# Two-layer hybrid decoder trunk on one core: column vectors of the second layer summed by VectorE, four products in place of sixteen transposes, and eight units in place of four kept back at the end

## The chip, the cores and the metric

The kernel runs on one core of a Trainium2 chip. A core has a matrix engine (TensorE, PE in the profile, with its weight loads as PEld), three engines for elementwise work (VectorE or DVE, ScalarE or ACT, GpSimd or POOL) and SyncE (SP), which issues most of the DMA transfers. Every engine has an instruction row of its own and works through it in order; the engines meet at semaphores only. The metric is the device time of one execution in microseconds (us): of the kernel before there are three runs with a median of 2212.91, from 2211.6 to 2215.46.

## The reference

Two layers over 256 tokens of 2048 numbers, all float32. Layer 0 mixes tokens with forgetting attention, layer 1 with windowed attention; each mixer is followed by a gated feed-forward part with 5632 columns. Before each of the four parts the tokens are modulated by a scale and a shift, and behind it the output is multiplied by a gate, added and normalised. Scales, shifts and gates come from one conditioning vector `c` through one large weight per layer (2048 x 12288, 100 MB each). The change touches these.

```python
def reference(x, c, ..., ada_w, ada_b, ...):
    c_act = jax.nn.silu(c)
    for i in range(DEPTH):                                   # DEPTH = 2
        mod = c_act @ ada_w[i] + ada_b[i]
        sh1, sc1, g1, sh2, sc2, g2 = jnp.split(mod[:, None, :], 6, axis=-1)
        h = x * (1.0 + sc1) + sh1
        y = fox_attention(h, ...) if i % 2 == 0 else swa_attention(h, ...)
        x = layer_norm(DEEPNORM_ALPHA * x + (1.0 + g1) * y, ln_mix_g[i], ln_mix_b[i])
        h = x * (1.0 + sc2) + sh2
        y = conv_ffn(h, ...)
        x = layer_norm(DEEPNORM_ALPHA * x + (1.0 + g2) * y, ln_ffn_g[i], ln_ffn_b[i])
    return x
```

## The kernel before

**Units.** All large weights stream through the core once, in pieces of 256 rows x 512 columns (512 KB); the text calls a piece a unit, and there are 728: 96 + 32 for layer 0's mixer (input and output projection), 264 for its feed-forward part (to U392), 40 + 32 for layer 1's mixer (to U464), 264 for the last feed-forward part. Each unit takes four steps. SyncE issues its load into `w` (L265, ten buffers in the pool that it shares with other loads). ScalarE copies it to `wh` in a type of fewer bits that TensorE multiplies faster (CAST, L268). VectorE subtracts to get the rest, `wl = w - wh` (L279). TensorE then multiplies three times, `wh` with the high part of the tokens, `wl` with the high part, `wh` with the low part (all from L75), which together give nearly the accuracy of float32. `wh` and `wl` have four buffers each.

With the tokens stationary (`x_mm`), a unit is twelve products of 512 columns: for each half of the tokens (t = 0 and 1, 128 tokens each) and each 128 rows, three. That is the form in the output and down projections, into the PSUM tiles `xs`. With the weights stationary (`w_mm`), a unit is 24 products of 256 columns (tiles `ws`).

**The background: conditioning vectors.** Ten of the twelve vectors of scales, shifts and gates are made beside the stream, in the order of `ada_list`: (layer, number) with numbers 0 and 1 for the mixer's shift and scale, 2 for its gate, 3 and 4 for the feed-forward part's, 5 for its gate. Each takes 32 loads `wa` of 128 x 1024 (L391) and 32 multiply-adds on VectorE into `acc` (L395 for the first, L397 for the rest), which leave 128 partial sums for each of the 2048 columns. How fast this goes is set by a rate: `ada_tick` adds the rate once per unit and takes one step of the generator `ada_vector` (to its next `yield`) for each whole number; `ada_need` takes all steps that are left when a vector is needed. What is left to do with `acc` depends on the vector:

- A gate is needed as a row in all partitions. It is split into `ah` and `al` (L84, L85), multiplied by ones, and copied into `gate`.
- A scale or shift is needed as a column block `cv` of 128 x 16. TensorE transposes the sixteen 128 x 128 blocks of `acc` in four groups of four (L439, `sm<-ident,acc`), ScalarE sums each transposed block along its row into `tot` (L443, sixteen accumulations), and VectorE adds the bias (L425). The four steps of four blocks are a `yield` apart; there are five yields in all. So are the columns of (1,0), (1,1), (1,3) and (1,4) made, and two of layer 0.

**Turns between parts.** `between` stands after each part: it waits for the vectors that the next part needs, merges the norm's weights into them, normalises the tokens (L655 on ScalarE for t = 0, L657 on VectorE for t = 1), transposes them (L496) and modulates them into `hH` and `hL`. The residual before it is L632 (product times gate), L634 (add to `x`), L639, L642, L644 (statistics), L645 (power -1/2 on GpSimd) and L638. TensorE waits for this chain at each turn. The text calls the one between layer 0 and layer 1 (after U392) the first turn, and the one between layer 1's output projection and its feed-forward part (after U464) the second.

**The end of a projection.** `x_mm_end` changes the order in the last n units: their products for t = 0 run first, the units are kept, and the products for t = 1 follow for all n. So the residual and the statistics of t = 0 can run beside the rest. n is 2 in layer 0's last down projection and 4 in layer 1's. Behind the latter stands the end of the program: eight normalising steps for each half (L1180, L1181) and the stores (L1182).

**What sets the order.** The program is written as one stream of units with steps put between them (`then`, `defer`, `run_post`, `tick`). The framework then orders each engine's row; what is wrapped in `pin` keeps its order against the other pinned instructions.

Of the kernel before, what the change touches and what calls it, by code (L numbers as in the profile page):

```python
# [10 lines left out]
F32 = mybir.dt.float32  # L11
F32R = mybir.dt.float32r
I32 = mybir.dt.int32
AF = mybir.ActivationFunctionType
ALU = mybir.AluOpType
# [26 lines left out]
def hybrid_trunk(ctx: ExitStack, tc: tile.TileContext, a: dict, out: bass.AP):  # L42
# [22 lines left out]
    def bank(name="sm"):  # L65
        return psp.tile([P, 512], F32, tag="ps", name=name)
# [66 lines left out]
    onesr = cst.tile([P, P], F32R, name="onesr")  # L133
    nc.vector.tensor_copy(onesr, ones)

    NF = 2 * DFF // P
    HR = ROPE_DIM // 2
    lcol = cst.tile([P, 4, DEPTH, KC], F32, name="lcol")
# [36 lines left out]
    def rotary():  # L175
# [2 lines left out]
        posr = tp.tile([NT, P], I32, tag="t", name="posr")  # L178
        nc.gpsimd.dma_start(posr, a["positions"].rearrange("b (t p) -> (b t) p", p=P))
        yield  # L180
        nc.vector.tensor_scalar_mul(nsink, sink, -1.0)
        posf = tp.tile([NT, P], F32, tag="t", name="posf")
        nc.vector.tensor_copy(posf, posr)
# [31 lines left out]
    def then(fn, alone=False):  # L215

        if alone:
            lone.add(fn)
        work.append(fn)
        if len(work) == 1 and not ahead[0]:  # L220
            settle()
# [35 lines left out]
        while post:  # L257
            run_post()

    def stream(wsrc, row0, col, ks, use):  # L260

        for kc in ks[::2]:
            r0 = (row0 + kc) * P
            w = wtile()
            pin(nc.sync.dma_start(w, wsrc[r0:r0 + 2 * P, col:col + WB].rearrange("(k p) f -> p k f", p=P)), False)  # L265
            h = hl.tile([P, 2, WB], F32R, tag="wh", name="wh")
            l = hl.tile([P, 2, WB], F32R, tag="wl", name="wl")
            pin(nc.scalar.copy(h, w), False)  # L268

            def go(kc=kc, h=h, l=l):  # L270
                ahead[0] -= 1
                run_post()
                use(kc, h, l)
                if feeds:
                    feeds.pop(0)()
                tick()

            def residual_(w=w, h=h, l=l, go=go):
                pin(nc.vector.tensor_tensor(l, w, f32(h), op=ALU.subtract), behind[0] > 0)  # L279
                behind[0] -= 1  # L280
                del residuals[go]

            ahead[0] += 1
            weights.add(go)
            residuals[go] = residual_
            work.append(go)
            settle(2)
# [25 lines left out]
    def w_mm(ps, kc, h, l, last=KC - 1, first=0):  # L313

        for i in range(2):
            for f in range(4):
# [3 lines left out]
                mm(o, wh, hL[:, kc + i, :], skip_group_check=True)  # L320
                mm(o, wl, hH[:, kc + i, :], stop=kc + i == last, skip_group_check=True)

    def x_stationary(wsrc, col, k0, nk, stat, end=0):

        ps = x_banks()
        use = x_mm_end(ps, stat, nk, end) if end else lambda kc, h, l: x_mm(ps, kc, h, l, stat, nk - 1)
        stream(wsrc, k0, col, list(range(nk)), use)
        return ps

    def w_stationary(wsrc, col):  # L330
# [42 lines left out]
    def ada_vector(l, v):  # L373
# [55 lines left out]
        if (l, v) in HELD:  # L429
            held.append((sums, finish))  # L430
            ada["held"] = not HELD[l, v]
            ready_cols.add((l, v))
        else:

            tot = sp.tile([P, KC], F32, tag="tot", bufs=1, name="tot")
            for k in range(0, KC, 4):
# [38 lines left out]
    def ada_need(l, v):  # L475
        while (l, v) not in cols and (l, v) not in gates and (l, v) not in ready_cols:
            ada_step()
# [272 lines left out]
    def out_proj(oT, full, w_o, l):  # L750
# [9 lines left out]
            stream(w_o, 0, d * WB, ks, use)  # L760

        for i, ks in enumerate((range(0, 8), range(8, 12))):
            then(lambda i=i: ada.update(rate=(1.3, 0.65)[l]))
            for d in range(2):
                part(d, list(ks))
        then(lambda: (ada_need(l, 2), ada.update(rate=(1.3, 0.75)[l])))
        for d in range(D // WB):
            if d < 2:
                part(d, list(range(12, KC)))
# [316 lines left out]
    def conv_ffn(l):  # L1086
# [37 lines left out]
        for si, (b0, b1) in enumerate(sbs):  # L1124
# [19 lines left out]

            then(ready)
            for d in range(D // WB):
                ps = x_stationary(w_dn, d * WB, b0 * 4, (b1 - b0) * 4, stat, (2, 4)[l] if si > 0 and d == D // WB - 1 else 0)
                then(lambda ps=ps, d=d, si=si: defer(residual(ps, d, gates[l, 5], si == len(sbs) - 1)),
                     si > 0 and d == D // WB - 1)
        then(lambda: (flush(), ada.update(gate_free=True)), True)  # L1150
# [58 lines left out]
```

## Time and profile before

| what | value |
|---|---|
| runs: median (lowest to highest) | 2212.91 us (2211.6 to 2215.46), 3 runs |
| profiled execution, device time | 2215.89 us |
| its span | 2214.0 us |
| TensorE busy | 2164.3 us, 98% |
| VectorE busy | 1792.8 us, 81% |
| ScalarE busy | 1159.6 us, 52% |
| GpSimd busy | 19.0 us, 1% |
| data moved by DMA | 602.98 MB, mean 272 GB/s |
| granted TensorE clock | 0.992 of full speed |

The span is the time between the first and the last instruction that the profile shows. A busy share is an average over the whole program; what counts for a change is the stretch in which it stands. Lines such as `1464.83 0.39 PE L75 MATMUL xs<-wh,hH 128*128 128x512 f32 x1` are read: start in us from the span's begin, duration, engine, line of the kernel, operation, output and inputs by the program's names, sizes, and how many of the kind in a row are put together. `[0.83 <-DVE mv L644]` says how long the engine had been idle ahead of it and which instruction ended that.

### The profile page before, as it was taken

Reading aid. Unit: us, or ns where it says so; the run is one execution under the profiler, and the core shown is the slowest. Engines: PE = TensorE matmul, PEld = TensorE weight load, DVE = VectorE, ACT = ScalarE, POOL = GpSimd, SP = SyncE. Lnnn points to the kernel's source line nnn. Section 1 sums busy time; section 2 is a strip of 40 time slices with the busy share of each in tenths; the row PEclk is TensorE's granted clock in tenths of the full one; section 3 lists DMA queues with packets and bytes.
Section 4 is the critical chain, followed back from the end, with each engine's and each line's share of the span. In section 5 each row is a group of like instructions: output and inputs, shape, how many; then the busy total and the mean of one; then the engine's idle time right before and its main releaser. Section 6 shows DMA issues by size and latency. Waiting matters only on the chain. (4 is left out here: it accounts for less than half of the span.)

```text
span 2214.0 us, 38357 instructions
## 1 busy us (share of the span) xinstructions
PE 2164.3 (98%) x14915; PEld 1976.7 (89%) x14915; DVE 1792.8 (81%) x2459; ACT 1159.6 (52%) x1841; POOL 19.0 (1%) x48
## 2 busy tenths in 40 slices
PE   6999999999999999999999999999999999999997
PEld 5999888789999988999987877789999988999986
DVE  6879998989978979799798888789888655666756
ACT  3435656465565543655644677555555533555532
POOL 0000000000000000000000000000000000000000
PEclk9999999999999999999999999999999999999999
DMA  9999998979978989899797676678888566666663
GB/s 334 368 352 366 351 352 298 327 257 323 349 234 300 322 312 385 260 311 322 251 354 290 201 240 206 208 257 295 281 264 270 187 194 195 192 195 195 191 195 108
DMA packets 274246, 602.98 MB, mean 272 GB/s; under 512 B 21062, under 2 KB 29960, under 8 KB 273552
## 3 DMA queue, kind: packets, MB, share of 16 engines
q1 hardware_dynamic: 273008, 595.85, 79.6%
q0 software_dynamic: 1056, 4.69, 0.6%
q8 instruction: 116, 1.90, 0.3%
q14 instruction: 66, 0.54, 0.1%
HBM read 598.37 MB, written 2.10 MB: 271 GB/s over the span
## 5 line engine op out<-in xcount | busy, mean ns | idle before, releaser
L268 ACT CAST wh<-w 128x1024 fp32r<-128x1024 f32 x728 | 765.3, 1053 | 790.0 <-PE ws L75 284.5
L75 PE MATMUL ws<-hH,wh 128*128 128x256 f32 x6656 | 1153.3, 278 | 4.6 <-ACT hH L84 2.1
L279 DVE TENSOR_TENSOR wl<-w,wh 128x1024 fp32r<-128x1024 f32 x728 | 887.6, 1222 | 325.3 <-ACT wh L268 308.5
L75 PEld LDWEIGHTS ws<-hH,wh 128*128 128x128 f32 x6656 | 1012.1, 189 | 9.0 <-ACT hH L84 2.3
L75 PE MATMUL ws<-hH,wl 128*128 128x256 f32 x3328 | 918.6, 277 | 4.3 <-DVE wl L279 4.0
L75 PEld LDWEIGHTS ws<-hH,wl 128*128 128x128 f32 x3328 | 628.5, 189 | 6.0 <-DVE wl L279 5.9
L75 PE MATMUL xs<-wh,gT 128*128 128x512 f32 x1408 | 435.3, 389 | 0.0
L75 PEld LDWEIGHTS xs<-wh,gT 128*128 128x128 f32 x1408 | 264.3, 188 | 54.7
L75 PE MATMUL xs<-wl,gT 128*128 128x512 f32 x704 | 273.9, 389 | 0.0
L75 PE MATMUL xs<-wh,hH 128*128 128x512 f32 x704 | 235.9, 401 | 0.0
L397 DVE SCALAR_TENSOR_TENSOR acc<-wa,cact,acc 128x1024 f32<-128x1024 f32 x180 | 228.4, 1278 | 0.0
L397 DVE SCALAR_TENSOR_TENSOR acc<-wa,cactp,acc 128x1024 f32<-128x1024 f32 x128 | 162.3, 1278 | 0.3 <-DMA acc<-in_ada_b_dram 0.3
L75 PEld LDWEIGHTS xs<-wh,hH 128*128 128x128 f32 x704 | 131.3, 188 | 29.4 <-issue 0.7
L75 PEld LDWEIGHTS xs<-wl,gT 128*128 128x128 f32 x704 | 132.2, 188 | 27.4
L75 PE MATMUL xs<-wl,hH 128*128 128x512 f32 x352 | 138.7, 395 | 2.5 <-DVE wl L279 2.5
L1093 ACT ACTIVATE u<-ws,ccol 128x256 f32<-128x256 f32 x176 | 96.7, 562 | 58.5 <-PE ws L75 43.3
L75 PE MATMUL xs<-wh,oT 128*128 128x512 f32 x384 | 126.2, 397 | 0.8 <-ACT oT L84 0.8
L1094 DVE SCALAR_TENSOR_TENSOR u<-ws,ccol,u 128x255 f32<-128x255 f32 x176 | 82.6, 477 | 14.9 <-ACT u L1093 14.7
L75 PEld LDWEIGHTS xs<-wh,oT 128*128 128x128 f32 x384 | 72.1, 188 | 16.6 <-ACT oT L84 1.2
L1096 DVE SCALAR_TENSOR_TENSOR u<-ws,ccol,u 128x254 f32<-128x254 f32 x176 | 83.1, 477 | 2.2
L75 PEld LDWEIGHTS xs<-wl,hH 128*128 128x128 f32 x352 | 66.5, 189 | 17.5 <-DVE wl L279 4.3
L576 DVE SCALAR_TENSOR_TENSOR oacc<-wo,cact,oacc 128x1024 f32<-128x1024 f32 (+1 forms) x68 | 73.3, 1078 | 8.3 <-DMA wo<-in_ada_w_dram 7.1
(220 smaller groups left out, 1280.4 us busy)
## 6 DMA issues: line engine op xcount, KB each, us to landing
w<-in_ffn_w_up_dram SPq DMA_DIRECT2D x352, 512.0 KB, 4.7
wa<-in_ada_w_dram SPq DMA_DIRECT2D x320, 512.0 KB, 5.6
w<-in_ffn_w_down_dram SPq DMA_DIRECT2D x176, 512.0 KB, 4.9
w<-in_fox_w_in_dram SPq DMA_DIRECT2D x96, 512.0 KB, 6.9
wo<-in_ada_w_dram SPq DMA_DIRECT2D x48, 512.0 KB, 9.0
w<-in_swa_w_in_dram SPq DMA_DIRECT2D x40, 512.0 KB, 4.6
w<-in_fox_w_o_dram SPq DMA_DIRECT2D x32, 512.0 KB, 6.2
w<-in_swa_w_o_dram SPq DMA_DIRECT2D x32, 512.0 KB, 4.8
```

What stands on the lines that cost most here:

```text
L75: return nc.tensor.matmul(o, lhsT, rhs, start=start, stop=stop, **kw)
L268: pin(nc.scalar.copy(h, w), False)
L279: pin(nc.vector.tensor_tensor(l, w, f32(h), op=ALU.subtract), behind[0] > 0)
L397: pin(nc.vector.scalar_tensor_tensor(ac, wo, (cactp if row else cact)[:, k:k + 1], ac, op0=ALU.mult, op1=ALU.add), True)
L576: nc.vector.scalar_tensor_tensor(acc, w[:, k], cact[:, kc:kc + 1], acc, op0=ALU.mult, op1=ALU.add)
L1093: nc.scalar.activation(u, pf, AF.Identity, bias=cw(CW, f), scale=cw(2, f))
L1094: nc.vector.scalar_tensor_tensor(u[:, 1:], pf[:, :S - 1], cw(1, f), u[:, 1:], op0=ALU.mult, op1=ALU.add)
L1096: nc.vector.scalar_tensor_tensor(u[:, 2:], pf[:, :S - 2], cw(0, f), u[:, 2:], op0=ALU.mult, op1=ALU.add)
```

## The change

There are four parts.

**Column vectors of layer 1.** For (1,0), (1,1), (1,3) and (1,4) the sixteen transposes on TensorE and the sixteen accumulations on ScalarE fall away. VectorE instead turns `acc` in place, in four pieces of 128 x 512: its transpose turns every 32 x 32 block within itself (L448 of the changed kernel). Two reductions of 128 x 1024 to 128 x 32 then sum each row of each block (L452) into `red`, 128 x 64. That leaves, for each column, four partial sums that stand 32 partitions apart and in a group of partitions of their own. Four float32 products with the stationary `fold` bring them together and put them in the partitions where `cv` has them, all into one bank of 128 x 16; the last line (L434) adds the bias, straight from the bank. A column vector has now seven yields behind its multiply-adds where it had five. Layer 0's two vectors stay as they were.

**`fold`.** A constant of 128 x 4 x 128, zeros (GpSimd's memset) and ones, made at the program's start by four small reductions of the identity on VectorE.

**Eight units at the end.** In layer 1's last down projection `x_mm_end` keeps eight of ten units. Eight pairs of `wh` and `wl` don't fit the four buffers, so four pairs are put in the region of `hH` and `hL`, which nobody reads any more at that place (`spares`).

**Rates.** In layer 1's output projection the background's rate is 0.75 per unit instead of 0.65 in its first part, and 1.1 instead of 0.75 behind that.

```diff
+    fold = cst.tile([P, 4, P], F32, name="fold")
+    nc.gpsimd.memset(fold, 0.0)
...
+        for q in range(4):
+            nc.vector.tensor_reduce(fold[:, q, q * 32:(q + 1) * 32], ident.rearrange("p (a i) -> p i a", a=4),
+                                    axis=AX.X, op=ALU.add)
...
-    def stream(wsrc, row0, col, ks, use):
+    def stream(wsrc, row0, col, ks, use, spare={}):
...
-            h = hl.tile([P, 2, WB], F32R, tag="wh", name="wh")
-            l = hl.tile([P, 2, WB], F32R, tag="wl", name="wl")
+            h, l = spare.get(kc) or (hl.tile([P, 2, WB], F32R, tag=n, name=n) for n in ("wh", "wl"))
...
+    def spares(nk):
+        t = [hpad[:, 56 + i * 2 * WB:56 + (i + 1) * 2 * WB].rearrange("p (a f) -> p a f", a=2) for i in range(8)]
+        return {nk - 16 + 2 * i: (t[2 * i], t[2 * i + 1]) for i in range(4)}
+
     def x_stationary(wsrc, col, k0, nk, stat, end=0):
...
-        stream(wsrc, k0, col, list(range(nk)), use)
+        stream(wsrc, k0, col, list(range(nk)), use, spares(nk) if end == 8 else {})
...
         else:
+
+            if l > 0:
+
+                for b in range(D // 512):
+                    r = acc[:, b * 512:(b + 1) * 512]
+                    nc.vector.transpose(r, r)
+                    yield
+                red = sp.tile([P, D // 32], F32, tag="red", bufs=1, name="red")
+                for b in range(2):
+                    nc.vector.tensor_reduce(red[:, b * 32:(b + 1) * 32],
+                                            acc[:, b * 1024:(b + 1) * 1024].rearrange("p (c j) -> p c j", j=32),
+                                            axis=AX.X, op=ALU.add)
+                    yield
+                tb = bank()
+                for q in range(4):
+                    mm(tb[:, :KC], fold[:, q, :], red.rearrange("p (k q) -> p q k", q=4)[:, q, :],
+                       start=q == 0, stop=q == 3)
+                yield
+                ps.append(tb)
+                finish()
+                ada["held"] = v == 4
+                return
 
             tot = sp.tile([P, KC], F32, tag="tot", bufs=1, name="tot")
...
-            then(lambda i=i: ada.update(rate=(1.3, 0.65)[l]))
+            then(lambda i=i: ada.update(rate=(1.3, 0.75)[l]))
...
-        then(lambda: (ada_need(l, 2), ada.update(rate=(1.3, 0.75)[l])))
+        then(lambda: (ada_need(l, 2), ada.update(rate=(1.3, 1.1)[l])))
...
-                ps = x_stationary(w_dn, d * WB, b0 * 4, (b1 - b0) * 4, stat, (2, 4)[l] if si > 0 and d == D // WB - 1 else 0)
+                ps = x_stationary(w_dn, d * WB, b0 * 4, (b1 - b0) * 4, stat, (2, 8)[l] if si > 0 and d == D // WB - 1 else 0)
```

The change adds lines, so that the same statement has another number behind it: the multiply-add L397 is L406, the subtraction L279 is L284, the residual's L632, L634, L639, L642, L644 and L638 are L663, L665, L670, L673, L675 and L669, the normalising L657 is L688, and the end's L1180 and L1181 are L1211 and L1212. Three places in VectorE's row show what moves.

The first is the last residual of layer 0, at the first turn; `xs` is the projection's bank, `mv` and `rs` the statistics of a half. Before:

```order
L632 TENSOR_TENSOR t<-xs,gate 128x512
L634 TENSOR_TENSOR x<-x,t 128x512
L639 BN_STATS stats<-x 128x6
L642 BN_AGGR mv<-stats 128x2
L644 TENSOR_SCALAR mv<-mv 128x1
L632 TENSOR_TENSOR t<-xs,gate 128x512
L634 TENSOR_TENSOR x<-x,t 128x512
L638 SCALAR_TENSOR_TENSOR rs<-mv,rs 128x1
L639 BN_STATS stats<-x 128x6
L642 BN_AGGR mv<-stats 128x2
```

After:

```order
L663 TENSOR_TENSOR t<-xs,gate 128x512
L665 TENSOR_TENSOR x<-x,t 128x512
L406 SCALAR_TENSOR_TENSOR acc<-wa,cactp,acc 128x1024
L670 BN_STATS stats<-x 128x6
L663 TENSOR_TENSOR t<-xs,gate 128x512
L673 BN_AGGR mv<-stats 128x2
L665 TENSOR_TENSOR x<-x,t 128x512
L675 TENSOR_SCALAR mv<-mv 128x1
L85 TENSOR_TENSOR al<-acc,ah 128x512
L669 SCALAR_TENSOR_TENSOR rs<-mv,rs 128x1
L670 BN_STATS stats<-x 128x6
L673 BN_AGGR mv<-stats 128x2
```

A multiply-add of the gate (1,2) and the first `al` of its split now stand inside this chain, and the two halves are woven into each other.

The second is layer 1's output projection, where the sums of (1,4) run. Before:

```order
L639 BN_STATS stats<-x 128x6
L397 SCALAR_TENSOR_TENSOR acc<-wa,cact,acc 128x1024
L634 TENSOR_TENSOR x<-x,t 128x512
L279 TENSOR_TENSOR wl<-w,wh 128x1024
L639 BN_STATS stats<-x 128x6
L397 SCALAR_TENSOR_TENSOR acc<-wa,cact,acc 128x1024
L279 TENSOR_TENSOR wl<-w,wh 128x1024
L397 SCALAR_TENSOR_TENSOR acc<-wa,cact,acc 128x1024
L279 TENSOR_TENSOR wl<-w,wh 128x1024
L397 SCALAR_TENSOR_TENSOR acc<-wa,cact,acc 128x1024
L279 TENSOR_TENSOR wl<-w,wh 128x1024 x2
```

After:

```order
L670 BN_STATS stats<-x 128x6
L406 SCALAR_TENSOR_TENSOR acc<-wa,cact,acc 128x1024
L665 TENSOR_TENSOR x<-x,t 128x512
L284 TENSOR_TENSOR wl<-w,wh 128x1024
L670 BN_STATS stats<-x 128x6
L406 SCALAR_TENSOR_TENSOR acc<-wa,cact,acc 128x1024 x2
L284 TENSOR_TENSOR wl<-w,wh 128x1024
L406 SCALAR_TENSOR_TENSOR acc<-wa,cact,acc 128x1024
L284 TENSOR_TENSOR wl<-w,wh 128x1024
L406 SCALAR_TENSOR_TENSOR acc<-wa,cact,acc 128x1024
L284 TENSOR_TENSOR wl<-w,wh 128x1024
L406 SCALAR_TENSOR_TENSOR acc<-wa,cact,acc 128x1024
```

Between two subtractions there are now two multiply-adds at one place, and one between all others, so that the vector's sums stand earlier among the units.

The third is the program's end. Before:

```order
L279 TENSOR_TENSOR wl<-w,wh 128x1024 x5
L632 TENSOR_TENSOR t<-xs,gate 128x512
L634 TENSOR_TENSOR x<-x,t 128x512
L639 BN_STATS stats<-x 128x6
L642 BN_AGGR mv<-stats 128x2
L644 TENSOR_SCALAR mv<-mv 128x1
L1180 SCALAR_TENSOR_TENSOR x<-x,mv,ln 128x512 x2
L1181 SCALAR_TENSOR_TENSOR x<-x,rs,ln 128x512 x2
L1180 SCALAR_TENSOR_TENSOR x<-x,mv,ln 128x512
L632 TENSOR_TENSOR t<-xs,gate 128x512
L1181 SCALAR_TENSOR_TENSOR x<-x,rs,ln 128x512
L634 TENSOR_TENSOR x<-x,t 128x512
```

After:

```order
L284 TENSOR_TENSOR wl<-w,wh 128x1024 x3
L663 TENSOR_TENSOR t<-xs,gate 128x512
L665 TENSOR_TENSOR x<-x,t 128x512
L670 BN_STATS stats<-x 128x6
L673 BN_AGGR mv<-stats 128x2
L675 TENSOR_SCALAR mv<-mv 128x1
L1211 SCALAR_TENSOR_TENSOR x<-x,mv,ln 128x512 x2
L1212 SCALAR_TENSOR_TENSOR x<-x,rs,ln 128x512 x2
L1211 SCALAR_TENSOR_TENSOR x<-x,mv,ln 128x512 x2
L1212 SCALAR_TENSOR_TENSOR x<-x,rs,ln 128x512 x2
L663 TENSOR_TENSOR t<-xs,gate 128x512
L665 TENSOR_TENSOR x<-x,t 128x512
```

All eight normalising steps of the first half (t = 0) now stand ahead of the second half's last residual; before, a part of them stood there.

## The prediction

> **What bounds the kernel now.** I read the page first (busy shares, granted clock), then the busy time in windows of 20 us, then the groups by form, and last the timeline at the five places that the change touches. All times are us.
>
> ```profile
> PE 2164.3 (98%) x14915; PEld 1976.7 (89%) x14915; DVE 1792.8 (81%) x2459; ACT 1159.6 (52%) x1841; POOL 19.0 (1%) x48
> ...
> PEclk9999999999999999999999999999999999999999
> ```
>
> TensorE is the bound, at full clock. The windows say where it has company; their columns are the stretch, its length, then busy time and instruction count of PE, PEld, DVE, ACT, POOL, then clock, DMA share and GB/s:
>
> ```profile
> 780.00:800.00 20.00, 20.00 (x97) 16.52 (x97) 12.68 (x13) 11.98 (x34) 0.00 (x0) 1.00 0.89 323
> 900.00:920.00 20.00, 20.00 (x178) 20.00 (x177) 12.55 (x16) 13.68 (x38) 0.00 (x0) 1.00 0.73 233
> 1080.00:1100.00 20.00, 20.00 (x174) 19.87 (x174) 10.40 (x13) 11.90 (x28) 0.58 (x1) 1.00 0.71 237
> 1200.00:1220.00 20.00, 18.66 (x85) 14.22 (x85) 14.75 (x28) 11.65 (x16) 1.10 (x2) 1.00 0.31 100
> 1420.00:1440.00 20.00, 20.00 (x90) 16.57 (x89) 20.00 (x23) 8.30 (x8) 0.00 (x0) 1.00 0.76 246
> ```
>
> At 780, 900 and 1080, where the sums of three of the four column vectors stand, TensorE has no gap and VectorE has 7 to 9 us free. At 1200 (first layer to second) TensorE waits. At 1420 (second layer's output projection) both are full. So a product taken off TensorE at the first three is worth its whole time there; at the last two it depends on VectorE.
>
> **The change, part by part.** "Unit" below is one weight piece of 512 KB: one CAST, one L279 subtraction, twelve 512-column products.
>
> *Turned sums off TensorE.* Four vectors lose 16 TensorE transposes each (L439), in groups of four. What one group costs, and the price list for VectorE:
>
> ```profile
> 1464.83 0.39 PE L75 MATMUL xs<-wh,hH 128*128 128x512 f32 x1
> 1465.06 0.60 PE L439 MATMUL sm<-ident,acc 128*128 128x128 f32 x4
> 1465.41 0.48 PE L75 MATMUL xs<-wh,hH 128*128 128x512 f32 x1
> ```
> ```profile
> L279 DVE TENSOR_TENSOR wl<-w,wh 128x1024 fp32r<-128x1024 f32 x728 | 887.6, 1222 | 325.3 <-ACT wh L268 308.5 <-DMA w<-in_ffn_w_down_dram 5.9 <-DMA wa<-in_ada_w_dram 5.8
> L397 DVE SCALAR_TENSOR_TENSOR acc<-wa,cact,acc 128x1024 f32<-128x1024 f32 x180 | 228.4, 1278 | 0.0
> L632 DVE TENSOR_TENSOR t<-xs,gate 128x512 f32<-128x512 f32 x48 | 32.1, 686 | 15.5 <-PE xs L75 15.3
> L705 DVE CUSTOM_DVE_ANT_0 pr<-S,mask,nsink 128x128 f32<-128x128 f32 x32 | 11.0, 345 | 0.0
> ```
>
> A product starts 0.23 after the one before it (1464.83 to 1465.06), so a unit of twelve takes about 2.7. The group pushes the next product back by 0.35 (1465.06 to 1465.41) and stretches it by 0.09 (0.48 against 0.39): 0.44. Of the 16 groups the last of the fourth vector came after the projection's last product, where TensorE waits anyway; 15 x 0.44 = **-6.6**. ScalarE's 64 accumulations go too, and cost nothing but at the second turn below.
>
> *Four small products per vector.* 16 in all, f32, 128x128 stationary, 16 columns. No such form is in the trace; the nearest is the one-column sum:
>
> ```profile
> 78.69 1.84 PE L75 MATMUL cps<-ones,oacc 128*128 128x1 f32 x16
> 80.40 0.25 PE L75 MATMUL cps<-cact,wo 128*128 128x1 f32 x1
> ...
> 20.63 1.87 PE L75 MATMUL cps<-ones,oacc 128*128 128x1 f32 x8 [0.51 <-DVE oacc L576]
> ```
>
> (80.40 - 78.69) / 16 = 0.107 each at speed, 1.87 / 8 = 0.234 in the opening. A group of four is 0.43, and I add 0.1 for the stretched product behind it, as with the transposes: 4 x 0.53 = **+2.1**; ends 1.7 and 16 x 0.234 = 3.7. I take the low row since these products stand in the running stream. [...]
>
> *Turned blocks and row sums on VectorE*, 4 + 2 per vector. Not in the trace. The turned block (128x512) I take as the 0.69 of L632, the row sum (128x1024) as the 1.22 of L279, which have the same columns: 4 x 0.69 + 2 x 1.22 = 5.2 per vector. The low end is nothing, the high end the dearest per column among the wide rows, L705 with 345 / 128 = 2.7 ns: 1.38 and 2.76, 11.0 per vector. The first three vectors have 7.3, 7.5 and 9.6 of VectorE time free (windows above), so 5.2 is hidden; the fourth is counted with the projection. The four reductions that build `fold` stand between the first loads of the program, where VectorE waits for DMA; 0.
>
> *Order: first layer's end.* Each vector now yields twice more, so the gate vector's sums end later. The order puts one L397 (L406 now) and one `al` subtraction into VectorE's row between the two halves' residuals, ahead of the statistics. The tail before:
>
> ```profile
> 1206.20 0.69 DVE L634 TENSOR_TENSOR x<-x,t 128x512 f32<-128x512 f32 x1
> ...
> 1207.95 0.15 DVE L644 TENSOR_SCALAR mv<-mv 128x1 f32<-128x1 f32 x1
> 1208.20 0.69 DVE L632 TENSOR_TENSOR t<-xs,gate 128x512 f32<-128x512 f32 x1
> ...
> 1209.54 0.15 DVE L638 SCALAR_TENSOR_TENSOR rs<-mv,rs 128x1 f32<-128x1 f32 x1
> ...
> 1210.68 0.15 DVE L644 TENSOR_SCALAR mv<-mv 128x1 f32<-128x1 f32 x1
> 1211.50 1.92 DVE L657 TENSOR_SCALAR x<-x,mv,rs 128x512 f32<-128x512 f32 x4 [0.66 <-POOL rs L645]
> ```
>
> Replay: the L397 runs 1206.8 to 1208.1 behind L634, so the second L632 starts at 1208.6 instead of 1208.20; the first L644 moves from 1207.95 to 1210.0 since three instructions of the other half now stand before it; then `al` to 1210.8; L638 must wait for GpSimd's power, which starts after L644 and so is ready at about 1210.9; L639 to L644 follow, and L657 starts at 1212.85. Behind it wait the x transposes, and TensorE: **+1.35**. Ends: 0.4 (only the later L632) and 2.0 (L397 and `al` in full).
>
> *Order: second layer's projection.* With the rates 0.75 and 1.1 the (1,4) vector's pieces come sooner.
>
> ```profile
> 1420.29 0.68 DVE L632 TENSOR_TENSOR t<-xs,gate 128x512 f32<-128x512 f32 x1
> ...
> 1434.39 1.27 DVE L397 SCALAR_TENSOR_TENSOR acc<-wa,cact,acc 128x1024 f32<-128x1024 f32 x1
> 1435.58 1.22 DVE L279 TENSOR_TENSOR wl<-w,wh 128x1024 fp32r<-128x1024 f32 x1
> ```
> ```profile
> 1438.47 0.39 PE L75 MATMUL xs<-wl,oT 128*128 128x512 f32 x1
> ```
>
> From 1420.29 VectorE runs without a gap to the subtraction of 1435.58, whose result TensorE reads first at 1438.47: 1.67 in hand. Up to that subtraction the order now holds two more L397 (1.19 from its start to the next, 1434.39 to 1435.58), and one before the residuals that makes them 0.35 later: its end moves from 1436.80 to 1439.3, past 1438.47: TensorE waits **+0.9**. After it the subtractions regain ground (one L397 and one subtraction take 2.3, a unit of TensorE 2.7); the turned blocks and row sums then stand among six subtractions, the tightest of which ends about 0.5 before it is needed. Ends: 0, if the row starts 0.9 sooner, and 3, if sums cost 1.5 each more and that 0.5 goes too.
>
> *Second turn.*
>
> ```profile
> 1472.30 0.15 DVE L644 TENSOR_SCALAR mv<-mv 128x1 f32<-128x1 f32 x1
> 1472.55 0.56 POOL L645 TENSOR_TENSOR rs<-mv,mhalf 128x1 f32<-128x1 f32 x1 [0.83 <-DVE mv L644]
> ...
> 1473.56 0.18 DVE L425 SCALAR_TENSOR_TENSOR cv<-tot,acol 128x16 f32<-128x16 f32 x1 [1.10 <-ACT sm L443]
> 1473.65 0.54 DVE L657 TENSOR_SCALAR x<-x,mv,rs 128x512 f32<-128x512 f32 x1
> ```
>
> L657 stood behind L425, which waited for ScalarE's last accumulation. The vector is now finished before the projection ends, and L657 can follow the power as at the first turn (0.82 after L644 started): 1473.12, **-0.5**. Next in line is the power itself.
>
> *Eight units kept.* Half the tokens finish early; what is left when TensorE ends:
>
> ```profile
> 2194.78 0.69 DVE L632 TENSOR_TENSOR t<-xs,gate 128x512 f32<-128x512 f32 x1 [3.13 <-PE xs L75]
> ...
> 2197.25 0.15 DVE L644 TENSOR_SCALAR mv<-mv 128x1 f32<-128x1 f32 x1
> ...
> 2199.11 0.62 PE L75 MATMUL xs<-wh,gT 128*128 128x512 f32 x2
> ...
> 2199.79 0.39 PE L75 MATMUL xs<-wh,gT 128*128 128x512 f32 x1
> ...
> 2200.63 0.68 DVE L632 TENSOR_TENSOR t<-xs,gate 128x512 f32<-128x512 f32 x1
> ...
> 2204.77 0.15 DVE L644 TENSOR_SCALAR mv<-mv 128x1 f32<-128x1 f32 x1
> ...
> 2208.82 1.41 DVE L1181 SCALAR_TENSOR_TENSOR x<-x,rs,ln 128x512 f32<-128x512 f32 x2
> ```
>
> Three products take 2199.79 - 2199.11 = 0.68, a kept unit's second half (six) 1.36. The first half now ends 8 x 1.36 = 10.9 before TensorE's last product instead of 5.4. It needs 2.6 (L632 to L644) and eight normalising steps of about 0.66, 5.3, so it is done with over 2 to spare. Then the second half's L632 starts with the last product's end (2200.2, not 2200.63) and reaches the end of L644 in 2.6 plus 0.1 for L638: 2202.9 instead of 2204.92, and what follows is unchanged: **-2.0**. The first halves consume weights at 1.36 per unit, above VectorE's 1.22; four of the eight pairs lie in the dead `hH` area and are cast ahead, so I cost that at 0. Without that cover up to 1.36 per late unit would be lost.
>
> Sum: -6.6 + 2.1 + 1.35 + 0.9 - 0.5 - 2.0 = **-4.75**. The profiled execution took 2215.89 (span 2214.0 and 1.89 around it), 2.98 over the median of the runs, 2212.91; I put the difference on the median: **2208.2**.
>
> **The rivals.**
> *VectorE late in the projection, or the end not gained.* For it: the full window at 1420. Against it: the row regains ground. With 3 in place of 0.9 the sum is -2.65, 2210.3; without the -2.0 it is -2.75, 2210.2. Within 0.2% either way.
> *Dear turned blocks and row sums; slower.* At the fourth vector every microsecond beyond 0.5 added to its four turned blocks and two row sums is TensorE's. At the high end, 11.0 instead of 5.2, that is 5.3 lost and 2213.5, no change; the kernel becomes slower by 0.2% (4.4) only if the six cost some 15 instead of 5.2, so about threefold. [...]
> *Cheaper than summed.* The first turn at 0.4 and no wait in the projection: -6.6, 2206.3.
> *A late load in the first turn.* Loads are held by buffers:
>
> ```profile
> 1197.66 20.47 SPq L265 DMA_DIRECT2D w<-in_swa_w_in_dram  x4
> ```
>
> Had the L397 in the tail to wait for its piece, the statistics would wait too; but its load stands about seven before these four. I leave it inside the first rival.
>
> **How the numbers follow.** About 0.2% (4.4) is what a measurement of this kernel can tell from no change. The summed case 0.60 (its spread crosses that bound: 0.48 beyond it, 0.12 within), the cheaper one 0.10, less gained 0.22, slower 0.08: faster 0.58, same 0.34, slower 0.08. Low end: no wait, 0.4 at the turn, products 1.7: -7.0, 2205.9, and from it the 1.3 by which the fastest run shown (2211.6) lies below the median: 2204.5. High end: products 3.7, turn 2.0, wait 3: -0.4, 2212.5.
>
> **What would show it.** After the change: no L439 after 500 and 16 products of 16 columns near 0.11; turned blocks near 0.69, row sums near 1.22; L657 at the first turn 1.3 later after TensorE's last product than before, at the second 0.5 sooner; one wait of TensorE near 1.0 for a `wl` in the projection; the chain's last part 8 after TensorE's last product instead of 10. The prediction is wrong if turned blocks take over 1.4, if `wl` waits exceed 3, or if TensorE waits in the last eight units.

## The result, and the profile after

The changed kernel takes 0.9987 of the time before, with a 95% interval of 0.9981 to 0.9993: medians of 2210.65 us (21 runs, 2208.81 to 2214.61) and 2215.11 (21 runs beside them, 2211.28 to 2219.55). By the ratio that is 2.9 us less, between 1.6 and 4.2: faster, but by less than the 0.2% that the prediction set as its bound, and by less than its 4.75. (The medians lie 4.5 apart and the means 3.5; the text goes by the ratio, since it comes with an interval.) The profiled execution took 2210.2 (span 2208.4).

Page of the changed kernel, busy time by engine, then the windows (columns as in the prediction):

```profile
PE 2158.4 (98%) x14883; PEld 1970.1 (89%) x14883; DVE 1810.2 (82%) x2487; ACT 1138.4 (52%) x1713; POOL 20.0 (1%) x49
```
```profile
780.00:800.00 20.00, 20.00 (x90) 16.58 (x89) 16.74 (x18) 7.39 (x7) 0.00 (x0) 1.00 0.90 309
900.00:920.00 20.00, 20.00 (x179) 20.00 (x178) 18.88 (x23) 10.59 (x14) 0.00 (x0) 1.00 0.82 270
1420.00:1440.00 20.00, 18.99 (x84) 15.38 (x83) 20.00 (x22) 6.66 (x7) 0.00 (x0) 1.00 0.84 260
```

VectorE filled up by 4 to 6 us where the first two vectors are summed, and TensorE still has no gap there; at 1420 TensorE now lacks 1.01. The new VectorE operations (durations in ns, least, median, most):

```profile
L448 DVE STREAM_TRANSPOSE acc<-acc x16: 669/704/709, 783.8 to 1450.8; 128x512 f32<-128x512 f32 x16
L452 DVE TENSOR_REDUCE red<-acc x8: 1177/1210/1216, 789.9 to 1454.9; 128x32 f32<-128x1024 f32 x8
```

That is 4 x 0.70 + 2 x 1.21 = 5.2 per vector, as summed. To see where time went, both traces are cut where TensorE changes over: the first group of idle-time products (`spin`) of each turn starts directly behind the last product of the part before. Timeline of the kernel before at the three turns and at its last product:

```profile
471.14 2.10 PE L75 MATMUL spin<-mask,ident 128*128 128x384 f32 x6
...
1208.01 2.10 PE L75 MATMUL spin<-mask,ident 128*128 128x384 f32 x6
...
1470.06 2.10 PE L75 MATMUL spin<-mask,ident 128*128 128x384 f32 x6
...
2199.79 0.39 PE L75 MATMUL xs<-wh,gT 128*128 128x512 f32 x1
```

And of the changed one:

```profile
468.78 2.10 PE L75 MATMUL spin<-mask,ident 128*128 128x384 f32 x6
...
1202.55 2.10 PE L75 MATMUL spin<-mask,ident 128*128 128x384 f32 x6
...
1467.15 2.10 PE L75 MATMUL spin<-mask,ident 128*128 128x384 f32 x6
...
2196.27 0.39 PE L75 MATMUL xs<-wh,gT 128*128 128x512 f32 x1
```

| stretch (us) | before | after | difference |
|---|---|---|---|
| start and layer 0's mixer, to 471.14 | 471.1 | 468.8 | -2.4 |
| layer 0's feed-forward part, three column vectors | 736.9 | 733.8 | -3.1 |
| first turn and layer 1's mixer | 262.1 | 264.6 | **+2.5** |
| second turn and last feed-forward part | 729.7 | 729.1 | -0.6 |
| last product to the end of the span | 14.2 | 12.1 | -2.1 |

The first row is not the change's alone: in the thirteen traces of this study the start took from 465.7 to 471.1 us. The four others repeat: a second trace of the changed kernel has them within 0.25 of the first. They add up to -3.3, inside the 1.6 to 4.2 of the measured ratio.

### The profile page after: what moved, and what is told of

Same layout as the page of the kernel before. It is cut to its first block, busy times and chain, and to the rows that moved or that the text cites. A ratio compares the mean times of both kernels' runs of the same rounds, so it can differ in the third digit from the quotient of the medians.

```text
span 2208.4 us, 38187 instructions
## 1 busy us (share of the span) xinstructions
PE 2158.4 (98%) x14883; PEld 1970.1 (89%) x14883; DVE 1810.2 (82%) x2487; ACT 1138.4 (52%) x1713; POOL 20.0 (1%) x49
## 4 chain that ended last, share of the span: by engine, by line
PE 82%; DVE 10%; issue 3%; ACT 2%; DMA 2%; SPq 0%; POOL 0%; DVEq 0%; ACTq 0%; POOLq 0%
PE ws L75 46%; PE xs L75 32%; DVE acc L406 3%; DVE wl L284 3%; DMA wo<-in_ada_w_dram 1%; ACT wh L273 1%; DMA w<-in_fox_w_in_dram 1%; PE sm L527 1%; PE cps L75 1%; DVE oacc L607 1%; PE S L75 1%; DVE pr L736 0%; PE sm L75 0%; PE o L75 0%; ACT pr L740 0%
## 5 line engine op out<-in xcount | busy, mean ns | idle before, releaser
L284 DVE TENSOR_TENSOR wl<-w,wh 128x1024 fp32r<-128x1024 f32 x724 | 881.7, 1220 | 300.2 <-ACT wh L273 274.0
L75 PE MATMUL xs<-wh,gT 128*128 128x512 f32 x1376 | 425.2, 389 | 0.0
L75 PEld LDWEIGHTS xs<-wh,gT 128*128 128x128 f32 x1376 | 258.3, 188 | 53.7
L75 PE MATMUL xs<-wl,gT 128*128 128x512 f32 x688 | 267.7, 389 | 0.0
L406 DVE SCALAR_TENSOR_TENSOR acc<-wa,cact,acc 128x1024 f32<-128x1024 f32 x180 | 227.9, 1276 | 0.0
L406 DVE SCALAR_TENSOR_TENSOR acc<-wa,cactp,acc 128x1024 f32<-128x1024 f32 x128 | 162.2, 1276 | 0.6 <-DMA acc<-in_ada_b_dram 0.6
```

Of the source, the lines that this page charges most:

```text
L75: return nc.tensor.matmul(o, lhsT, rhs, start=start, stop=stop, **kw)
L406: pin(nc.vector.scalar_tensor_tensor(ac, wo, (cactp if row else cact)[:, k:k + 1], ac, op0=ALU.mult, op1=ALU.add), True)
```

## The experiments

The theory after this comparison: the time is the sum of the parts, and the gain was eaten at three places, by the four products, by the first turn, and by a wait for `wl` in layer 1's output projection (the wait is there, but not for `wl`: see the old rates). Rivals are given with each.

**The end alone.** The kernel before, with the eight kept units.

```diff
-  ... (2, 4)[l] if si > 0 and d == D // WB - 1 else 0)
+  ... (2, 8)[l] if si > 0 and d == D // WB - 1 else 0)     (with spares(), as in the change)
```

> The kernel before with the eight kept units (and the four pairs in the dead region) alone. Distance from the start of TensorE's last product to the end of the span: 14.25 us before, 12.14 after. Theory (the end is a part of its own, worth what its chain of waits shows): 12.1 here too, no wait of TensorE in the last ten units, everything ahead as before, so 2.1 faster, a ratio of 0.9990. Rival (the eight units make TensorE or VectorE wait for buffers, and the two traces differ there by the start of the program only): the distance falls to 12.1, but TensorE's products of the last ten units take over 1 us longer than before, and the time does not change.

Ratio 0.9994 (0.9985 to 1.0003). TensorE's last product and the last normalising steps in its timeline:

```profile
2199.08 0.39 PE L75 MATMUL xs<-wh,gT 128*128 128x512 f32 x1
```
```profile
2199.51 0.69 DVE L635 TENSOR_TENSOR t<-xs,gate 128x512 f32<-128x512 f32 x1 [2.94 <-PE xs L75]
...
2206.03 1.41 DVE L1184 SCALAR_TENSOR_TENSOR x<-x,rs,ln 128x512 f32<-128x512 f32 x2
```

From the last product to the end of the span (2211.3) it is 12.2, the stretch ahead of it 729.75 against 729.73: the end is worth 2.1 and costs nothing. VectorE had idled 2.94 before the last residual, so it is not late. The ratio alone is too wide to show 0.1%; the trace does.

**Five steps per vector.**

```diff
                     nc.vector.transpose(r, r)
-                    yield
+                    if b % 2:
+                        yield
```

> The changed kernel, but the four turned blocks are made two per step, so that a column vector has five steps behind its sums as it had before. Theory (the first turn is later because the gate's last multiply-add and its split fell into it): at the first turn L657's counterpart starts 6.0 after the first of the two last residual products, as before, not 7.6; 1.55 faster than the changed kernel, the rest the same. Rival (the turn is later since the two halves of the statistics are woven into each other by the scheduler, whatever the gate does): it stays above 7.0.

Ratio 0.9974 (0.9965 to 0.9982). VectorE at the first turn, in the changed kernel and in this one:

```profile
1200.02 0.69 DVE L663 TENSOR_TENSOR t<-xs,gate 128x512 f32<-128x512 f32 x1 [1.93 <-PE xs L75]
1200.75 0.69 DVE L665 TENSOR_TENSOR x<-x,t 128x512 f32<-128x512 f32 x1
1201.36 1.28 DVE L406 SCALAR_TENSOR_TENSOR acc<-wa,cactp,acc 128x1024 f32<-128x1024 f32 x1
...
1204.54 0.68 DVE L85 TENSOR_TENSOR al<-acc,ah 128x512 fp32r<-128x512 f32 x1
1205.68 0.16 DVE L669 SCALAR_TENSOR_TENSOR rs<-mv,rs 128x1 f32<-128x1 f32 x1 [0.46 <-POOL rs L676]
...
1207.59 1.91 DVE L688 TENSOR_SCALAR x<-x,mv,rs 128x512 f32<-128x512 f32 x4 [0.67 <-POOL rs L676]
```
```profile
1200.93 0.69 DVE L664 TENSOR_TENSOR t<-xs,gate 128x512 f32<-128x512 f32 x1 [3.13 <-PE xs L75]
...
1206.95 1.92 DVE L689 TENSOR_SCALAR x<-x,mv,rs 128x512 f32<-128x512 f32 x4 [0.66 <-POOL rs L677]
```

7.57 from the residual's start to the normalising, against 6.02 here and 6.02 before (1211.50 - 1205.48): the 1.55 is the gate's doing. The weaving of the halves came and went with it, so this run can't price the two apart. By the ratios this kernel is 2.9 faster than the changed one, with intervals that touch; by its trace 2.0 (1.55 at the turn, 0.4 in the mixer).

**The old rates.**

```diff
-            then(lambda i=i: ada.update(rate=(1.3, 0.75)[l]))
+            then(lambda i=i: ada.update(rate=(1.3, 0.65)[l]))
...
-        then(lambda: (ada_need(l, 2), ada.update(rate=(1.3, 1.1)[l])))
+        then(lambda: (ada_need(l, 2), ada.update(rate=(1.3, 0.75)[l])))
```

> The changed kernel with the background's old rates of 0.65 and 0.75 in the second layer's output projection. Theory (TensorE's wait for wl there comes from the rates, which put one more multiply-add ahead of that subtraction): TensorE's idle time of 1.0 near the sixth unit after the attention (unit 454) goes, 1.35 of time with the restart; the turned blocks and row sums come in the last units, and the four products come behind the projection's last product, where TensorE waits anyway, another 0.9; the second turn gets up to 0.5 longer. Sum: 1.5 to 2.2 faster than the changed kernel. Rival (the wait comes from the turned blocks and row sums, VectorE being full there): the idle time moves to the last units and stays at 1 or more, and the time is that of the changed kernel or longer.

The wait first, in the changed kernel, on VectorE, TensorE and ScalarE:

```profile
1432.73 2.46 DVE L406 SCALAR_TENSOR_TENSOR acc<-wa,cact,acc 128x1024 f32<-128x1024 f32 x2
1435.11 1.22 DVE L284 TENSOR_TENSOR wl<-w,wh 128x1024 fp32r<-128x1024 f32 x1
```
```profile
1434.72 0.84 PE L75 MATMUL xs<-wh,oT 128*128 128x512 f32 x3
1436.58 0.74 PE L75 MATMUL xs<-wh,oT 128*128 128x512 f32 x2 [1.01 <-ACT wh L273]
1437.16 0.40 PE L75 MATMUL xs<-wl,oT 128*128 128x512 f32 x1
```
```profile
1435.48 1.04 ACT L273 CAST wh<-w 128x1024 fp32r<-128x1024 f32 x1 [1.99 <-DMA w<-in_swa_w_o_dram]
```

The subtraction of unit 454 ends at 1436.33, and the theory took it for what TensorE waits for. It isn't. The profile names a CAST, and the CAST of 1435.48, the program's 457th, ends at 1436.53, 0.05 before TensorE goes on at 1436.58. TensorE's row has changed along with VectorE's: from 1434.95 on it has four products with `wh` ahead of unit 454's first with `wl` (1437.16), where the kernel before has one (1438.24, the second of the two in the first line):

```profile
1438.02 0.61 PE L75 MATMUL xs<-wh,oT 128*128 128x512 f32 x2
1438.47 0.39 PE L75 MATMUL xs<-wl,oT 128*128 128x512 f32 x1
```

So products of later units stand there, and by the times one of them needs the `wh` of unit 457. The kernel with five steps, which has the same row, tells the two causes apart; ScalarE, VectorE and TensorE there:

```profile
1434.42 1.05 ACT L273 CAST wh<-w 128x1024 fp32r<-128x1024 f32 x1 [1.66 <-PE xs L75]
```
```profile
1434.35 1.22 DVE L284 TENSOR_TENSOR wl<-w,wh 128x1024 fp32r<-128x1024 f32 x1
```
```profile
1435.52 0.73 PE L75 MATMUL xs<-wh,oT 128*128 128x512 f32 x2 [0.68 <-ACT wh L273]
```

TensorE goes on at 1435.52, 0.05 after that CAST and before the subtraction ends (1435.57). The 0.05 is the same in all five traces with these rates. Here ScalarE had idled 1.66 before that CAST, until TensorE freed a buffer, as before nearly every CAST around it, and TensorE's wait is 0.68; in the changed kernel it idled 1.99, until a load landed, which is the other 0.33 of the 1.01. The late `wl` that the theory meant is there as well, but behind this: in its old place, at 1435.18, its first product would have waited an estimated 1.15 (1436.33 - 1435.18).

With the old rates the same window reads:

```profile
1420.00:1440.00 20.00, 20.00 (x90) 16.53 (x90) 20.00 (x23) 8.46 (x8) 0.00 (x0) 1.00 0.75 243
```

The wait is gone with VectorE just as full, and TensorE's row is that of before again, so the rates made it, by way of TensorE's row, and not the turned blocks. But the ratio is 0.9989 (0.9980 to 0.9998), no better than the changed kernel's 0.9987. The trace has something that no theory had named, and that would account for it if it comes in most executions, which isn't shown. Windows of 4 us behind the first turn, of this kernel and of the changed one; the third column from the right is TensorE's granted clock:

```profile
1207.00:1211.00 4.00, 2.64 (x10) 1.94 (x11) 3.27 (x9) 3.39 (x6) 0.55 (x1) 0.64 0.00 0
1211.00:1215.00 4.00, 4.00 (x10) 2.52 (x10) 4.00 (x9) 1.33 (x3) 0.00 (x0) 0.51 0.00 0
```
```profile
1207.00:1211.00 4.00, 3.20 (x18) 2.21 (x16) 3.41 (x9) 3.54 (x7) 0.55 (x1) 1.00 0.00 0
1211.00:1215.00 4.00, 4.00 (x23) 3.31 (x22) 4.00 (x8) 2.07 (x4) 0.00 (x0) 1.00 0.04 9
```

The clock fell to half for some 6 us, with the same turn, the same order and the same idle time ahead of it. Lined up unit by unit, that cost 2.65 in this trace. Without it the stretch from first to second turn is 265.6 - 2.65 = 262.9 against the changed kernel's 264.6, and the next one, with a second turn whose column vector is late again, 0.2 longer: 1.45 gained, just under the expected range.

**One product for four.**

```diff
-                for q in range(4):
-                    mm(tb[:, :KC], fold[:, q, :], red.rearrange("p (k q) -> p q k", q=4)[:, q, :],
-                       start=q == 0, stop=q == 3)
+                mm(tb[:, :D // 32], fold, red, start=True, stop=True)
...
+                for q in range(4):
+                    o = slice(q * 32, (q + 1) * 32)
+                    (cv[o] = column 4k + q of tb[o] + acol[o])
```

> The changed kernel with one float32 product of 64 columns in place of four of 16 (the stationary holds four copies of the 32x32 identity in each row of blocks, so every group of partitions gets all 64 sums, and four 32x16 additions of the bias pick what belongs to each). Theory (a float32 product is run as two passes of 0.107 whatever its few columns; the four cost 0.81 and 0.09 for the product behind): the one takes 0.21 to 0.25 and pushes TensorE's next product back by 0.2 to 0.35 instead of 0.81 to 0.9, 0.6 per vector, 2.3 faster than the changed kernel over the four; VectorE has three more additions of 0.17 per vector, hidden. Rival (the price goes by columns): 64 columns cost as much as four times 16, and nothing is gained.

A group of four in the changed kernel (timeline), and the one in the kernel of the sixth experiment, which has it too:

```profile
802.37 0.40 PE L75 MATMUL xs<-wh,gT 128*128 128x512 f32 x1
802.60 0.96 PE L75 MATMUL sm<-red,fold 128*128 128x16 f32 x8
803.41 0.47 PE L75 MATMUL xs<-wh,gT 128*128 128x512 f32 x1
```
```profile
796.68 0.33 PE L75 MATMUL sm<-red,fold 128*128 128x64 f32 x2
796.82 0.48 PE L75 MATMUL xs<-wh,gT 128*128 128x512 f32 x1
```

Four products are eight rows: the trace has two for each float32 product of this kind. (The idle-time products are float32 too: three of 384 columns are six rows in 2.10, 0.70 each, where a product of 512 columns with `wh` starts 0.23 after the one before it.) The eight push the next product back by 0.81 and stretch it by 0.08, 0.89 in all; the two by 0.14 and 0.09, 0.23, although they have four times the columns. Layer 0's feed-forward part is 1.96 shorter than in the changed kernel (731.84 against 733.8), 0.65 per vector, as expected. The ratio is 0.9983 (0.9975 to 0.9992) where 2.3 less would be 0.9977. In the trace the clock fell behind the first turn here too (0.60 over 1204 to 1208, 0.54 over 1208 to 1212), and the wait in the projection was 1.48: the stretch there is 267.2.

**The sums alone.** Turned blocks, row sums, four products, five steps; old rates, four kept units (the edits above together).

> The column sums alone: turned blocks, row sums and four products, in five steps per vector, with the old rates and four kept units. Theory (sum by parts): the feed-forward part of layer 0 3.1 shorter (729.58 us from its first products to its last in the profile before); the first turn unchanged at 7.39 with the clock at 1.00; the second layer's mixer, 254.24 from the first turn to its last product, 1.1 to 1.5 shorter, since its last vector's transposes are gone and the four products come after the last product; the second turn 8.05 as before; the end as before. 4.2 to 4.6 faster than before, ratio 0.9980. Rival (VectorE's added 20 us make TensorE wait for wl wherever VectorE is full): the mixer is not shorter than before, and the ratio is 0.9986 or more.

Ratio 0.9962 (0.9950 to 0.9975), 8 us. The trace outside the start gives 5.4: 3.1 in layer 0, 1.1 in the mixer, 1.15 behind. So the sums do pay, by 0.8 to 1.2 more than expected. 0.5 of that is the second turn (7.5 from the last product of 512 columns instead of 8.05); the last four products stand in it, where TensorE waits anyway.

```profile
1461.30 0.40 PE L75 MATMUL xs<-wh,hH 128*128 128x512 f32 x1
1461.54 0.96 PE L75 MATMUL sm<-red,fold 128*128 128x16 f32 x8
```

The rest of the 8 lies in the start (3.5 shorter in this trace) and in the spread of five runs; it isn't explained.

**All mended.** The changed kernel with five steps, one product, and rates of 0.70 and 0.85.

> The changed kernel with five steps per vector, one product of 64 columns, and rates of 0.70 and 0.85, so that fewer multiply-adds stand ahead of unit 454's subtraction while the column vector is still done before the projection's last residual. Theory: layer 0's feed-forward part 5.0 shorter than before; first turn 7.39, clock 1.00; the mixer 253.2 to 254.0; second turn 7.29; end 8.36 after TensorE's last product; in all 8.5 to 9.2 faster than before, ratio 0.9960, and 2.5 to 3.5 faster than with five steps alone. Rival (the wait for wl moves to another unit of the projection): the mixer stays at 255 or more and the ratio at 0.9967 or more.

Ratio 0.9946 (0.9933 to 0.9958), median 2201.94. The stretches are 731.8, 258.8, 729.1 and 12.1, 11.0 below before, where 8.5 to 9.2 was expected. TensorE has no wait in the window of the projection any more, and its row there is that of before; the excess is in the mixer, 251.4 by the measure of the expectation. Lined up by units it comes between units 438 and 448, 1.6 less than in the kernel before: there the end of the attention runs beside the multiply-adds, which the rate of 0.70 sets at other places of it. With 0.75 the changed kernel lost 0.55 there. Why one place is that much better was not tried.

```profile
1420.00:1440.00 20.00, 20.00 (x90) 16.57 (x89) 20.00 (x22) 7.54 (x8) 0.00 (x0) 1.00 0.92 305
```

> The kernel with five steps, one product of 64 columns and rates of 0.70 and 0.85 again, to narrow its ratio: 11.0 below before by the stretches of its trace outside the program's start, ratio 0.9950.

Again: 0.9939 (0.9927 to 0.9950), median 2199.95, and the same stretches to 0.1. It beats both kernels. The 11.0 of the stretches would be 0.9950, the edge of this interval; what is more isn't explained.

**Is it the length of the turn that lowers the clock?** The kernel before, with a longer first turn.

```diff
             nc.vector.tensor_tensor(xs, xs, tmp, op=ALU.add)
+            if t == 1:
+                for _ in range(late):          (5 at layer 0's last residual, else 0)
+                    nc.vector.tensor_scalar_mul(xs, xs, 1.0)
```

> The kernel before with the first turn made longer: x of the second half's last block is multiplied by 1.0 five times on VectorE ahead of its statistics (2.3 to 2.7 us), which changes no value. Theory (a turn that keeps TensorE idle longer makes the granted clock fall to 0.5 behind it, in some executions of the changed kernel, and here in most): the clock reads 0.50 for some 6 us behind the turn, and the turn with the products behind it grows by 2.5 + 2.6 = 5.1; ratio 1.0023. Rival (the fall in the traces of the old rates and of the single product came from something else that the changed kernel does there): the clock stays at 1.00, and the time grows by 2.5, ratio 1.0011.

And with more products that keep TensorE going:

```diff
-        spin(o, 3)
+        spin(o, 3 if v else 8)
```

> The same with eight idle-time products (spin) on TensorE instead of three at that turn, 0.5 each, so that TensorE works while VectorE is late. Theory: the clock stays at 1.00 and the time is before plus 2.5, ratio 1.0011, 2.6 less than without them. Rival (the clock falls whatever TensorE does there, or not at all): the same time as without them, or longer.

Ratios 1.0023 (1.0014 to 1.0032) and 1.0008 (0.9999 to 1.0017), as the theory said. The clock behind the turn, without and with:

```profile
1210.00:1214.00 4.00, 0.66 (x4) 0.42 (x4) 3.16 (x9) 2.08 (x3) 0.55 (x1) 0.99 0.00 0
1214.00:1218.00 4.00, 3.70 (x10) 2.59 (x11) 4.00 (x10) 2.78 (x6) 0.00 (x0) 0.58 0.00 0
```
```profile
1207.00:1211.00 4.00, 3.59 (x13) 1.98 (x11) 3.13 (x10) 1.92 (x3) 0.55 (x1) 1.00 0.00 0
1211.00:1215.00 4.00, 3.54 (x17) 2.67 (x18) 4.00 (x10) 2.94 (x6) 0.00 (x0) 1.00 0.00 0
```

The same 2.4 on VectorE costs 5.1 by the ratio where TensorE is left idle, and 1.8 where it isn't. From the first turn to the second, the two traces are 3.65 and 2.4 longer than before: in this one the clock was at half for 3.4 us and not for the 6 expected, which cost 1.25. Over their eleven runs each, the granted clock has a median of 0.991 without the added products and 0.994 with them, as in the kernel before beside them.

**Does it fall in the changed kernel itself?** Once more the changed kernel, and beside it with `spin(o, 3 if v else 6)`.

> The changed kernel once more, for a second trace of it. Theory (its first turn of 8.94 is near the length at which the clock falls, so that it falls in some executions and not in others): all stretches as in its first trace within 0.1 but the program's start and the first turn, which is either 8.94 again or, with the clock at 0.5 behind it, 2.65 longer with the products that follow; ratio to before 0.9985, and its runs spread over 4 us or more. Rival (the falls in the two variants' traces were theirs): the first turn as in the first trace, spread as that of before.

> The changed kernel with six idle-time products at the first turn instead of three. Theory: TensorE's idle stretch of 2.1 ahead of the first transposes of that turn shrinks to about 0.6, the clock stays at 1.00 in every execution, the turn stays at 8.9, and the mean of its runs is 0.8 to 1.9 below that of the unchanged one beside it (2.65 times a chance between 0.3 and 0.7). Rival (the clock does not fall in the changed kernel's own executions, or hardly): the same mean within 0.5.

Ratios 0.9988 (0.9979 to 0.9996) and 0.9991 (0.9982 to 1.0000), means of 2211.8 and 2211.9: no gain to be seen, against the theory, though intervals of 2 us to either side can't exclude one of 0.8 to 1.9. The trace of the changed kernel again has the clock at 1.00 there, and with more products the idle stretch of 2.1 is gone as meant:

```profile
1203.87 4.03 PE L75 MATMUL spin<-mask,ident 128*128 128x384 f32 x12
1208.05 0.66 PE L527 MATMUL sm<-ident,x 128*128 128x128 f32 x4
```

So with the changed kernel's turn the clock fell in two traces of four, both of variants. How often it does in the changed kernel's own runs stays open. Three of the twelve new runs stand apart, at 2215.7 to 2217.2 with a granted clock of 0.991; the other nine end by 2212.0 with 0.993 to 0.995, and none of the eleven with more products is below 0.992. That would fit a fall in a quarter of the runs, but these three weren't traced, and they lie 6 us above the mean of the nine, more than the fall at this turn cost in any trace.

## Why the prediction was right or wrong

The time lies in the range (2204.5 to 2212.5) and the sign is right; 0.13% lies in the bin of "within 0.2%", to which I gave 0.34, not in the likeliest. That the sum came within 2 us of the measured change is in part luck: two of its sizes stood on wrong readings, one of which came out near. The steps:

- *Transposes off TensorE, -6.6.* Right, a little small. The three vectors of layer 0's stretch and the four products there give -3.1 together; with 0.89 for a group of products that is 1.92 per vector, 0.48 per group instead of 0.44, -7.2 for fifteen.
- *Four small products, +2.1.* The failed step. I read `x16` and `x8` in the rows of the one-column products as so many products; they are so many rows, two to a product, as the changed kernel's `x8` for four products shows. 0.107 is right for a row and 0.214 for a product (0.81 / 4 = 0.20 in the group above): 0.89 three times and 0.81 at the fourth vector are +3.5. The mechanism, a fixed price whatever the few columns, held for those that ran: 0.107 a row with 1 column and, the next product's stretch included, 0.89 / 8 = 0.11 with 16 and 0.23 / 2 = 0.12 with 64. That the high end (3.7) covered it is luck: its 0.234 was a row of the opening, where the products of 256 columns start 0.21 apart, too (0.12 from 30 us on). At 0.234 a row, 16 products would have been 7.5.
- *Turned blocks and row sums, hidden.* Right, 0.70 and 1.21, where the rows of as many columns from which I took them had 0.69 and 1.22. The row sum is no dearer than the subtraction L284 of as many columns, 1.22 in the changed kernel too. The dear rival falls.
- *First turn, +1.35.* +1.55, by the instructions that the replay named. What it left out is the clock behind a longer idle time: in the windows of 4 us behind this turn it read 0.64 and 0.51 in the trace of the old rates, and 1.00 in that of the changed kernel.
- *Projection, +0.9.* Wrong in its mechanism, and near in size by luck. The wait came at the unit that the replay named, and was +1.35, of which 1.01 was idle time and the rest the restart. But the replay looked at VectorE's row alone and kept TensorE's as it was; the wait that ended last was for a CAST three units ahead. (By its own terms the replay gives 1436.80 + 2 x 1.19 + 0.35 = 1439.5 and a wait of 1.06, not 1439.3 and 0.9.) Besides, lined up by units, the multiply-adds that the new rates moved into the attention cost 0.55 there (units 440 to 448), and the late gate 0.2 behind the first turn; neither had a term.
- *Second turn, -0.5.* By its own measure right: L688 follows the last statistic (1469.83) at 1470.65, 0.82 as forecast. Up to where TensorE's stream runs again it is -0.77. The last feed-forward part gives another 0.27 that I can't place.

```profile
1469.83 0.15 DVE L675 TENSOR_SCALAR mv<-mv 128x1 f32<-128x1 f32 x1
1470.65 1.92 DVE L688 TENSOR_SCALAR x<-x,mv,rs 128x512 f32<-128x512 f32 x4 [0.67 <-POOL rs L676]
```

- *End, -2.0.* -2.1, and shown by itself.

With these sizes the sum is -7.2 + 3.5 + 1.55 + 1.35 + 0.75 - 0.77 - 0.27 - 2.1 = -3.2, where the stretches show -3.3. The rival "less gained" was the nearest, by its size; its mechanism, a wait of 3 or an end not gained, was not what happened.

## What to carry to other kernels

Count the rows of an instruction against the program before dividing by them: a price per row is not a price per product. A background job that is paced by steps ends later when it gets more steps, so look at what its end falls into; two steps more per vector took 2.0 us of the 5.2 that the changed kernel has without them. When the profile names the engine that ended a wait, look for the last instruction of that engine before the wait's end, also one that the program seems to need only later: a changed rate can reorder the row of the engine that waits. And where TensorE must wait for another engine, the wait can have a second price behind it, the clock: 0.58 over the 4 us from 1214 in the lengthened turn, and 1.25 us of time. Products that nobody needs took that price away there (1.00 in both windows); in the changed kernel they gained nothing that could be measured.

## What the runs showed of the hardware

The clock was not in the prediction at all. In all thirteen traces it fell at 41 to 44 us, in or behind a wait of TensorE of 4.4 to 6.7 us (in the kernel before 5.06, for VectorE's `oacc`, L576); over the 4 us from 44 to 48 it reads 0.50 in ten of them and 0.54, 0.64 and 0.66 in the others. In three it fell behind a first turn that has grown. From the end of the first idle-time products to the start of the second there are 2.5 us in the kernel before (1210.1 to 1212.6), and the clock fell in none of the six traces with that turn; 4.0 in the changed kernel (1204.7 to 1208.7), and it fell in two traces of four with that turn; 5.2 with the lengthened turn (1210.0 to 1215.2), and it fell in its trace. The traces show no fixed length of idle time behind which it falls: with the 4.0 it fell in one execution and not in another, and near 55 us, where TensorE has nothing but four transposes for 2.5 us (53.4 to 55.9 in the kernel before), it fell in eight of the thirteen, to 0.58 to 0.76 in the lowest window of 4 us of each.

A gap of TensorE isn't needed for the clock to fall. In the kernel before it fell at 81.2, where the records show no idle time of TensorE, while 32 rows of one-column products ran (78.69 to 83.05):

```profile
74.00:81.20 7.20, 7.20 (x65) 7.11 (x63) 3.99 (x4) 3.15 (x3) 0.00 (x0) 1.00 1.05 387
81.20:88.00 6.80, 6.80 (x32) 6.61 (x32) 4.61 (x7) 0.96 (x2) 0.00 (x0) 0.50 0.96 340
```

Twelve of the thirteen traces have such a fall between 79 and 164 us: in its lowest window of 4 us the clock reads 0.50 to 0.62, with TensorE busy for all of the 4 us. The idle-time products that kept the clock up in the lengthened turn have 384 columns; how narrow they may be was not tried.
